# Rows of the rounded x at 512 columns instead of 528, for the first of two blocks

## The chip, the cores and the metric

One core of one Trainium2 chip runs the whole program. The metric is the device time of one execution in microseconds (us); the median over several runs is compared. An engine is named as in the profile: PE is TensorE (its matmuls), PEld its weight loads, DVE is VectorE, ACT is ScalarE, POOL is GpSimd, SP the queue that issues most DMAs.

## The reference, cut to what matters

Two blocks of a network, one after the other, on 512 tokens of width 1024, everything in float32.

```
# first block
u = rmsnorm(h, g_mix);  z = u @ w_in            # 7440 columns
y_gla, y_conv, y_swa = three mixers of parts of z, each @ its own output matrix
h = h + (sigmoid(gates0)*y_gla + sigmoid(gates1)*y_conv + sigmoid(gates2)*y_swa) @ w_o
u = rmsnorm(h, g_ffn);  hid = causal_dwconv(u @ w_up, ffn_conv_w)   # 2 x 2816 columns
h = h + (silu(hid[:2816]) * hid[2816:]) @ w_down
x2 = rmsnorm(h, g_final)
# second block: 16 meta tokens set ahead of x2 (528 tokens), two other mixers, another FFN
```

## The kernel before, in words

The activations lie with the model dimension on the 128 partitions: x is eight k-tiles of 128 rows of the model dimension, and in each partition a k-tile is one row of tokens. A float32 product is made of three float32r products: each operand is split into a rounded high part and a low part (the rest), and `pass3` (L181 through `mm`) issues weights-high by x-high, weights-high by x-low, weights-low by x-high, all into one accumulator of 512 columns. `gemm` does that for each k-tile of one group of 128 output columns: 8 k-tiles x 3 = 24 matmuls with 512 moving columns, and an evacuation by DVE and ACT afterwards.

The rounded x lives in two buffers `XH` and `XL` of 8 rows x 528 columns (`L` = 512 tokens + 16 meta tokens). The first block uses 512 columns of each row, from column `X1` = 8 on. The second block uses all 528. So row k begins k x 2112 bytes after the first.

The weights come from one stream in the order of use (`WStream`): 1024 columns (8 tiles of 128 columns, 512 bytes each in a partition) in one DMA into `wraw`, then ACT casts them to `wh` (L83) and DVE writes the rest to `wl` (L84). Three buffers each of `wh` and `wl` (4096 bytes a partition), two of `wraw`.

The buffers are laid out in a partition in the order of their allocation. Between the start of `XH` and the start of the first `wh` buffer lie XH and XL (16896 bytes each), the parameters (2048), the constants (1632) and two `wraw` (4096 each): 45664 bytes, which is 89 x 512 + 96. All weight tiles are whole multiples of 512 bytes from that one. `MH`/`ML` (the merged mixers' output, split), `bh_*`/`bl_*` (the mixers' outputs, split) and `FH`/`FL` (the hidden layer of the FFN, split) have rows of 512 columns (2048 bytes); their starts, from the sizes of the tiles ahead of them, are whole multiples of 512 bytes from the weights. `MH` begins 131072 + 96 bytes after `XH`, and `ML` as much after `XL`.

The order of work of the first block: a first group of four output tiles with x as the stationary operand, then 30 gemms of `w_in` among which the mixers' small matmuls are woven (`Lane`, `tick`: generators that are advanced after each k-tile), then 8 rounds of 3 gate gemms (24 matmuls each) and 3 gemms of the mixers' output matrices (4 k-tiles, 12 matmuls each), then `w_o` (8 gemms that read `MH`, `ML`), then the FFN: 44 gemms of `w_up` that read `XH`, `XL` and 8 gemms of `w_down` (22 k-tiles each) that read `FH`, `FL`. In the evacuation of `w_down` the second block's x is written into `XH`, `XL` (`after`). The matmuls of x with 512 moving columns are thus 30 + 24 + 44 = 98 gemms of 24.

Of the kernel before, what the change touches and what calls it, by code (L numbers as in the profile page):

```python
# [10 lines left out]
F32R = mybir.dt.float32r  # L11
# [7 lines left out]
P = 128  # L19
D = 1024  # L20
T = 512
META = 16
L = T + META
PADL = T + 32
X1 = 8
KD = D // P
NFF = 22
EPS = 1e-6
# [99 lines left out]
class Builder:  # L128
# [177 lines left out]
    def setup(self):  # L306
        nc, c = self.nc, self.const
        self.H = c.tile([P, KD, L], F32, name="H")
        self.XH = c.tile([P, KD, L], F32R, name="XH")
        self.XL = c.tile([P, KD, L], F32R, name="XL")  # L310
        self.par_t = c.tile([P, NPAR], F32, name="par_t")
        cm = c.tile([P, 3 * P + 24], F32, name="cm")
        self.four = cm[:, 3 * P:3 * P + 16]
        self.ident, self.le, self.ones = (cm[:, i * P:(i + 1) * P] for i in range(3))
        nc.scalar.preload_act_table_set("exp_and_others")
        nc.sync.dma_start(out=self.H[:, 0, META:L], in_=self.ins["xT"][:, 0])
        nc.scalar.dma_start(out=self.par_t[:, 0:8], in_=self.ins["par"][:, 0:8])
        self.W.load_to(0)
        for k in range(1, KD):
            nc.sync.dma_start(out=self.H[:, k, META:L], in_=self.ins["xT"][:, k])  # L320
            if k == 2:
                self.W.load_to(1)
        nc.gpsimd.dma_start(out=self.par_t[:, 8:NPAR], in_=self.ins["par"][:, 8:NPAR])
        nc.gpsimd.dma_start(out=cm[:, 0:3 * P + 16], in_=self.ins["cm"])
        nc.gpsimd.dma_start(out=self.H[:, :, 0:META], in_=self.ins["metaT"])

    def X(self, c0=META):
        return lambda k: (self.XH[:, k, :], self.XL[:, k, :])

    def sumsq(self, acc, k, src):  # L330
        if k == 0:
# [169 lines left out]

    def block1(self):
        nc, tc = self.nc, self.tc
        H, XH, XL = self.H, self.XH, self.XL
        self.W.prep_to(0)
        sums = [self.sq_acc(), self.sq_acc()]

# [9 lines left out]
            self.act(t, h, AF.Square)  # L517
            eng.tensor_tensor(out=sums[k % 2], in0=sums[k % 2], in1=t, op=ALU.add)
        for k in range(KD):
            self.split(XH[:, k, X1:X1 + T], XL[:, k, X1:X1 + T], H[:, k, META:L], self.par("g_mix", k))  # L520
            if k > 2:
                square(k - 3)
        for k in range(KD - 3, KD):
# [1 line left out]
        Rt = self.stat.tile([P, 4], F32, tag="Rt", name="Rt", bufs=1)  # L525
        R = self.r_tile()
        Rx = R[:, META:L]
        segs = [(X1, T)]
        X = self.X()
        WI = lambda c: [("w_in", k, c) for k in range(KD)]  # L530

        with ExitStack() as s1:
# [10 lines left out]
            with ExitStack() as s2:  # L543
# [14 lines left out]
                with tc.tile_pool(reuse_waits="tile", name="sp", bufs=1) as sp:  # L558
                    self.dist = sp.tile([P, 256], F32, name="dist")
                    nc.gpsimd.dma_start(out=self.dist, in_=self.ins["dist"])  # L560
                    sk = sp.tile([P, T], F32, name="sk")
                    svt = sp.tile([P, 4, P], F32, name="svt")
                    sq = [sp.tile([P, T], F32, name=f"sq{t}") for t in range(4)]
                    accs = [self.acc() for _ in range(4)]
                    for k in range(KD):
                        wh, wl = self.W.take([("w_in", k, GV + m * P) for m in range(4)])
                        for b in range(4):
                            c = slice(X1 + b * P, X1 + (b + 1) * P)
                            for i, (x, w) in enumerate(((XH, wh), (XL, wh), (XH, wl))):
                                self.mm(accs[b], x[:, k, c], w, start=k == 0 and i == 0, stop=k == 7 and i == 2)  # L570
                        if k == 5:
                            self.norm(self.token_rstd(sums, D, R, META, Rt), 4)
                        self.tick(4)

                    def ev_gv(a):
                        for b in range(4):
                            self.act(self.GVt[:, b, :], a[b], AF.Copy, scale=Rt[:, b:b + 1])
                    self.pend.append((ev_gv, accs))
                    self.flush(2)
                    self.lanes[1].add(self.meta_norm(), 6)  # L580
                    self.gemm16(wga, self.par("g_mix", 0, KD), [(META, T)], 3,
                                lambda a: self.mul(self.GAt[0:96], a[0][0:96], Rx[0:96]))
                    self.gemm(WI(SK), X, segs, lambda a: self.mul(sk, a[0], Rx))
                    sv = sp.tile([P, T], F32, tag="pT", name="sv", bufs=2)

                    def sv_gen():
                        ps = self.sm()
                        for n in range(4):
                            self.tr(ps[:, n * P:(n + 1) * P], sv[:, n * P:(n + 1) * P])
                        nc.scalar.copy(svt.rearrange("p a b -> p (a b)"), ps)  # L590
                        yield 1
                    self.gemm(WI(SV), X, segs, lambda a: self.mul(sv, a[0], Rx))
                    self.lanes[0].add(sv_gen(), 3)
                    for t in range(4):
                        self.gemm(WI(("sq", t)), X, segs,
                                  lambda a, t=t: self.stt(sq[t], a[0], 0.125, Rx, ALU.mult, ALU.mult))
                    self.flush(0, 1)
                    self.lanes[0].add(self.swa(sp, sq, sk, svt), 3)
                    sgr = [br.tile([P, T], F32, tag=f"blg{i}", name=f"sgr{i}") for i in range(4)]
                    for h in range(4):  # L600
                        def ev_gr(a):
                            t = gp.tile([P, T], F32, tag="a1", name="gr", bufs=1)
                            self.mul(sgr[h], a[0], Rx)
                            self.act(t, sgr[h], AF.Sigmoid)
                            self.mul(sgr[h], sgr[h], t)
                        self.gemm(WI(GR + h * P), X, segs, ev_gr)
                    glas = []
                    for h in range(4):
                        q = gp.tile([P, T], F32, tag="q", name="q", bufs=2)
                        kk = gp.tile([P, T], F32, tag="kk", name="kk", bufs=2)  # L610
                        self.gemm(WI(GQ + h * P), X, segs,
                                  lambda a: self.stt(q, a[0], float(P) ** -0.5, Rx, ALU.mult, ALU.mult))
                        self.gemm(WI(GK + h * P), X, segs, lambda a: self.mul(kk, a[0], Rx))
                        self.lanes[2].add(self.gla_head(gp, h, q, kk, sgr[h]), 2)
                    self.flush(0, 1)
# [48 lines left out]
            for m in range(KD):  # L664
                def ev_o(a, m=m):
                    h = H[:, m, META:L]
                    self.add(h, h, a[0])
                    self.split(XH[:, m, X1:X1 + T], XL[:, m, X1:X1 + T], h, self.par("g_ffn", m))
                    self.sumsq(sqa, m, h)
                self.gemm([("w_o", k, m * P) for k in range(KD)], lambda k: (MH[:, k, :], ML[:, k, :]), [(0, T)], ev_o)  # L670
        R = self.r_tile()
# [2 lines left out]
        g1 = self.stat.tile([P, 8], F32, tag="g1", name="g1", bufs=1)  # L674
        nc.gpsimd.tensor_tensor(out=g1, in0=self.par("g_final", 0, 8), in1=self.par("norm1", 0, 8), op=ALU.mult)

        def after(m, h, _):
            self.split(XH[:, m, META:L], XL[:, m, META:L], h, g1[:, m:m + 1])
            self.split(XH[:, m, 0:META], XL[:, m, 0:META], H[:, m, 0:META], self.par("norm1", m))
            self.sumsq(sqh, m, h)  # L680
            self.ts(h, h, self.par("g_final", m), ALU.mult)
            self.sumsq(sqg, m, h)
# [3 lines left out]
    def ffn(self, up, cw, cb, down, R, after, zero):  # L686
        nc, tc, H = self.nc, self.tc, self.H
        W = T + 2
        segs = [(X1, T)] if zero else [(META - 2, 256), (META + 254, 258)]
        rsegs = [(META, T)] if zero else segs  # L690
        Xb = (self.XH, self.XL)
        with tc.tile_pool(reuse_waits="tile", name="fp", bufs=1) as fp:
            FH = fp.tile([P, NFF, T], F32R, name="FH")
            fp.tile([P, P], F32, name="pad3")
# [1 line left out]
            for j in range(NFF):  # L696
                cs = []
                for i in range(2):
                    f = j + NFF * i
                    u = fp.tile([P, W], F32, tag="u", name="u", bufs=2)  # L700
                    c = fp.tile([P, T], F32, tag=f"c{i}", name=f"c{i}", bufs=2 if i == 0 else 1)
# [3 lines left out]
                    def ev(a, i=i, f=f, u=u, c=c, cs=cs, j=j):  # L705
# [13 lines left out]
                        else:  # L719
                            self.mul(c, cs[0], c)  # L720
                            self.split(FH[:, j, :], FL[:, j, :], c)
                    self.gemm([(up, k, f * P) for k in range(KD)],
                              lambda k: (Xb[0][:, k, :], Xb[1][:, k, :]), segs, ev)
                    cs.append(c)
            for m in range(KD):
                def ev_d(a):
# [338 lines left out]

    def block2(self, sqh, sqg):
        nc, tc, st = self.nc, self.tc, self.stat
        H, XH, XL = self.H, self.XH, self.XL
        W2 = T + 2
        R = self.r_tile()  # L1070

# [22 lines left out]
        self.norm(norm2(), 10)  # L1094
        segs = [(0, 264), (264, 264)]
        segq = [(META - 2, 256), (META + 254, 258)]
        X = self.X()
        WI = lambda c: [("w_in_2", k, c) for k in range(KD)]

        with ExitStack() as sy:  # L1100
# [406 lines left out]
```

## Time and profile before

| what | value |
|---|---|
| median of 3 runs | 1769.63 us (1768.66 to 1769.98) |
| profiled execution, its own time | 1771.67 us |
| its span (first to last instruction) | 1769.8 us |
| PE busy | 1738.0 us (98%) |
| DVE busy | 1089.8 us (62%) |
| ACT busy | 729.7 us (41%) |
| DMA, mean | 91 GB/s |
| mean granted TensorE clock | 0.997 |

The busy time of PE is the union of its matmuls, which overlap: the end of one runs into the next. So the pace of a stage is read from the starts of its matmuls, not from their durations. Around the span lie 1.87 us that the profile does not place.

### The profile page before, as it was taken

The numbers are of one execution on the slowest core, as the hardware profiler recorded it, in microseconds if no ns is written. First come the engines' busy times: TensorE is split into PE (matmuls) and PEld (weight loads), VectorE is DVE, ScalarE is ACT, GpSimd is POOL, SyncE is SP. The second block draws the span as 40 slices with busy tenths as digits, with TensorE's granted clock in tenths as the row PEclk, the third lists the DMA queues.
The fourth block names the chain that finished last, engine by engine and source line by source line (L and its number), as shares of the span: only waits on it lengthen the run. The fifth ranks groups of instructions, "written<-read, shape, count | busy, mean of one in ns | idle before, by whom it ended". The sixth has DMA issues, their size and how long they took to land. (4 is left out here: it accounts for less than half of the span.)

```text
span 1769.8 us, 26970 instructions
## 1 busy us (share of the span) xinstructions
PE 1738.0 (98%) x11014; PEld 1534.6 (87%) x11014; DVE 1089.8 (62%) x1923; ACT 729.7 (41%) x1175; POOL 123.9 (7%) x203
## 2 busy tenths in 40 slices
PE   8999999999999999999998999999999999999997
PEld 6777778888888888888897999999999999999885
DVE  4476774444457777734488789767643667766332
ACT  4355443222344444433356545545432444444221
POOL 2000000000110000001112221000001000000000
PEclk9999999999999999999999999999999999999999
DMA  5222223332333333233333322122223223332331
GB/s 184 84 72 60 64 80 96 96 96 95 96 95 94 93 94 95 92 100 101 88 101 126 113 86 72 61 73 72 72 84 96 84 96 95 86 95 96 96 89 67
DMA packets 45691, 160.84 MB, mean 91 GB/s; under 512 B 5472, under 2 KB 5616, under 8 KB 45568
## 3 DMA queue, kind: packets, MB, share of 16 engines
q1 hardware_dynamic: 42480, 149.83, 27.3%
q0 software_dynamic: 2800, 9.03, 1.6%
q8 instruction: 86, 1.41, 0.3%
q14 instruction: 37, 0.30, 0.1%
q10 hardware_dynamic: 288, 0.27, 0.0%
HBM read 156.93 MB, written 2.18 MB: 90 GB/s over the span
## 5 line engine op out<-in xcount | busy, mean ns | idle before, releaser
L181 PE MATMUL acc<-XH,wh 128*128 128x512 f32 (+3 forms) x2320 | 633.2, 326 | 0.1
L181 PE MATMUL acc<-XL,wh 128*128 128x512 f32 (+3 forms) x2320 | 621.1, 321 | 0.0
L181 PE MATMUL acc<-XH,wl 128*128 128x512 f32 (+3 forms) x2320 | 619.0, 320 | 0.0
L83 ACT CAST wh<-wraw 128x1024 fp32r<-128x1024 f32 (+1 forms) x279 | 292.0, 1047 | 507.8 <-PE acc L181 441.8
L84 DVE TENSOR_TENSOR wl<-wraw,wh 128x1024 fp32r<-128x1024 f32 (+1 forms) x279 | 342.6, 1228 | 218.8 <-ACT wh L83 211.4
L181 PEld LDWEIGHTS acc<-XH,wh 128*128 128x128 f32 x2320 | 385.1, 189 | 45.2 <-issue 9.8
L181 PEld LDWEIGHTS acc<-XH,wl 128*128 128x128 f32 x2320 | 385.3, 189 | 33.8 <-issue 0.5
L181 PEld LDWEIGHTS acc<-XL,wh 128*128 128x128 f32 x2320 | 385.9, 189 | 32.9 <-issue 0.5
L181 PE MATMUL acc<-FH,wh 128*128 128x512 f32 x352 | 137.8, 392 | 0.0
L181 PE MATMUL acc<-FH,wl 128*128 128x512 f32 x352 | 137.1, 390 | 0.0
L181 PE MATMUL acc<-FL,wh 128*128 128x512 f32 x352 | 137.0, 389 | 0.0
L164 DVE SCALAR_TENSOR_TENSOR c<-u,par_t,c 128x512 f32<-128x512 f32 x176 | 131.8, 749 | 6.7 <-ACT c L178 3.7
L152 DVE TENSOR_TENSOR u<-acc,R 128x512 f32<-128x512 f32 (+2 forms) x132 | 63.8, 510 | 87.9 <-PE acc L181 84.7
L336 POOL TENSOR_TENSOR sqa<-sqa,sqt 128x512 f32<-128x512 f32 x27 | 40.8, 1513 | 735.5 <-ACT sqt L178 735.5
L181 PEld LDWEIGHTS acc<-FH,wl 128*128 128x128 f32 x352 | 66.1, 188 | 14.0
L181 PEld LDWEIGHTS acc<-FL,wh 128*128 128x128 f32 x352 | 66.1, 188 | 13.5
L181 PEld LDWEIGHTS acc<-FH,wh 128*128 128x128 f32 x352 | 66.1, 188 | 13.4
L178 ACT ACTIVATE FH<-c 128x512 fp32r<-128x512 f32 x44 | 27.8, 632 | 116.0 <-DVE c L152 116.0
L178 ACT ACTIVATE c<-u,par_t 128x512 f32<-128x512 f32 x88 | 67.6, 768 | 2.4 <-DVE u L152 2.2
L152 DVE TENSOR_TENSOR H<-H,acc 128x512 f32<-128x512 f32 (+2 forms) x41 | 22.6, 569 | 74.6 <-PE acc L181 74.6
L178 ACT ACTIVATE c<-c 128x512 f32<-128x512 f32 x44 | 27.8, 632 | 83.5 <-DVE c L164 83.5
L181 PE MATMUL acc<-yh,wh 128*128 128x256 f32 (+1 forms) x256 | 51.4, 282 | 0.1
(393 smaller groups left out, 1967.1 us busy)
## 6 DMA issues: line engine op xcount, KB each, us to landing
wraw<-in_wts SPq DMA_DIRECT2D x277, 512.0 KB, 3.6
seg<-cumd POOLq DMA_DIRECT2D x10, 512.0 KB, 4.3
H<-in_xT SPq DMA_DIRECT2D x8, 256.0 KB, 9.6
ei<-eid POOLq DMA_DIRECT2D x16, 128.0 KB, 3.3
out<-H SPq DMA_DIRECT2D x7, 256.0 KB, 2.7
wraw<-in_wts SPq DMA_DIRECT2D x2, 256.0 KB, 4.6
r<-in_r POOLq DMA_DIRECT2D x1, 272.0 KB, 3.2
r<-in_r POOLq DMA_DIRECT2D x1, 256.0 KB, 8.3
```

Of the source, the lines that this page charges most:

```text
L83: self.nc.scalar.copy(h[:, e], t[:, e])
L84: self.nc.vector.tensor_tensor(out=l[:, e], in0=t[:, e], in1=h[:, e].bitcast(F32), op=ALU.subtract)
L152: self.nc.vector.tensor_tensor(out=out, in0=a, in1=b, op=op)
L164: self.nc.vector.scalar_tensor_tensor(out=out, in0=a, scalar=s, in1=b, op0=op0, op1=op1)
L178: self.nc.scalar.activation(out=out, in_=a, func=func, scale=scale, **kw)
L181: self.nc.tensor.matmul(out, lhsT, rhs, start=start, stop=stop)
L336: self.nc.gpsimd.tensor_tensor(out=acc, in0=acc, in1=t, op=ALU.add)
```

## The change

The two buffers keep their place and size. For the first block they are seen as 8 rows of 512 columns, from column 24 of the flat buffer on (`self.X1`, rows of 2048 bytes, the first 96 bytes in); for the second block as before, 8 rows of 528 columns (`self.X2`). All users take the view that they need. No instruction is added or taken away.

```diff
-X1 = 8
+X1 = 24
...
-        self.XH = c.tile([P, KD, L], F32R, name="XH")
-        self.XL = c.tile([P, KD, L], F32R, name="XL")
+        self.X1, self.X2 = [], []
+        for n in ("XH", "XL"):
+            x = c.tile([P, KD * L], F32R, name=n)
+            self.X1.append(x[:, X1:X1 + KD * T].rearrange("p (k t) -> p k t", t=T))
+            self.X2.append(x.rearrange("p (k t) -> p k t", t=L))
...
-    def X(self, c0=META):
-        return lambda k: (self.XH[:, k, :], self.XL[:, k, :])
+    def X(self, x):
+        return lambda k: (x[0][:, k, :], x[1][:, k, :])
...
-            self.split(XH[:, k, X1:X1 + T], XL[:, k, X1:X1 + T], H[:, k, META:L], self.par("g_mix", k))
+            self.split(XH[:, k, :], XL[:, k, :], H[:, k, META:L], self.par("g_mix", k))
...
-        segs = [(X1, T)]
-        X = self.X()
+        segs = [(0, T)]
+        X = self.X(self.X1)
...
-                            c = slice(X1 + b * P, X1 + (b + 1) * P)
+                            c = slice(b * P, (b + 1) * P)
...
         def after(m, h, _):
-            self.split(XH[:, m, META:L], XL[:, m, META:L], h, g1[:, m:m + 1])
-            self.split(XH[:, m, 0:META], XL[:, m, 0:META], H[:, m, 0:META], self.par("norm1", m))
+            self.split(XH2[:, m, META:L], XL2[:, m, META:L], h, g1[:, m:m + 1])
+            self.split(XH2[:, m, 0:META], XL2[:, m, 0:META], H[:, m, 0:META], self.par("norm1", m))
...
-        segs = [(X1, T)] if zero else [(META - 2, 256), (META + 254, 258)]
+        segs = [(0, T)] if zero else [(META - 2, 256), (META + 254, 258)]
...
-        Xb = (self.XH, self.XL)
+        X = self.X(self.X1 if zero else self.X2)
```

`block2` takes `self.X2` everywhere.

## Rows read from the trace of the kernel before

**Rows 1.** Busy time and count of each engine in seven stretches (windows view)

```profile
0.00:38.60 38.60, 31.48 (x137) 22.89 (x137) 19.39 (x32) 21.67 (x31) 12.60 (x19) 1.00 0.59 198
38.60:258.90 220.30, 216.60 (x1145) 171.49 (x1144) 146.02 (x303) 100.04 (x204) 0.40 (x4) 1.00 0.23 72
258.90:458.20 199.30, 199.30 (x868) 162.18 (x867) 94.26 (x114) 58.29 (x71) 0.00 (x0) 1.00 0.31 95
458.20:501.70 43.50, 43.50 (x194) 36.03 (x193) 21.15 (x25) 17.09 (x24) 11.23 (x8) 1.00 0.31 97
501.70:748.20 246.50, 246.50 (x1073) 200.03 (x1072) 175.89 (x236) 107.92 (x141) 6.02 (x43) 1.00 0.30 94
748.20:867.90 119.70, 119.70 (x529) 99.09 (x528) 49.16 (x50) 37.21 (x46) 16.94 (x12) 1.00 0.31 97
867.90:1769.80 901.90, 880.93 (x7079) 842.86 (x7078) 583.96 (x1165) 387.48 (x661) 76.74 (x117) 0.99 0.28 88
```

**Rows 2.** Groups by form, whole span: one of three passes over x, first block

```profile
L181 PE MATMUL acc<-XH,wh 128*128 128x512 f32 x784 | 312.5, 399 | 0.0
```

**Rows 3.** Timeline of PE, two starts in w_up, 960 matmuls apart

```profile
514.69 0.39 PE L181 MATMUL acc<-XH,wh 128*128 128x512 f32 x1
...
737.09 0.39 PE L181 MATMUL acc<-XH,wh 128*128 128x512 f32 x1
```

**Rows 4.** Timeline of PE, two starts in w_o, 180 matmuls apart

```profile
458.84 0.39 PE L181 MATMUL acc<-MH,wh 128*128 128x512 f32 x1
...
499.64 0.39 PE L181 MATMUL acc<-MH,wh 128*128 128x512 f32 x1
```

**Rows 5.** Timeline of PE, start of w_down: matmuls 0, 4, 10 and 500

```profile
748.21 0.39 PE L181 MATMUL acc<-FH,wh 128*128 128x512 f32 x1
...
749.15 0.39 PE L181 MATMUL acc<-FL,wh 128*128 128x512 f32 x1
...
750.53 0.39 PE L181 MATMUL acc<-FL,wh 128*128 128x512 f32 x1
...
861.60 0.39 PE L181 MATMUL acc<-FH,wl 128*128 128x512 f32 x1
```

**Rows 6.** Timeline of PE, gate rounds: matmuls 0, 108, 120 and 144

```profile
300.59 0.39 PE L181 MATMUL acc<-bh_gla,wh 128*128 128x512 f32 x1
...
325.49 0.39 PE L181 MATMUL acc<-bh_gla,wh 128*128 128x512 f32 x1
...
328.26 0.39 PE L181 MATMUL acc<-bh_conv,wh 128*128 128x512 f32 x1
...
333.70 0.39 PE L181 MATMUL acc<-XH,wh 128*128 128x512 f32 x1
```

**Rows 7.** Timeline of PE, second block's w_down, after four small matmuls

```profile
1649.30 0.60 PE L184 MATMUL sm<-cm,H 128*128 128x128 f32 x4
...
1651.36 0.39 PE L181 MATMUL acc<-FL,wh 128*128 128x512 f32 x1
...
1654.99 0.39 PE L181 MATMUL acc<-FH,wl 128*128 128x512 f32 x1
```

**Rows 8.** Timeline of PE in w_in, first and last of 96 matmuls without small ones

```profile
53.10 0.48 PE L181 MATMUL acc<-XH,wh 128*128 128x512 f32 x1
...
75.22 0.39 PE L181 MATMUL acc<-XH,wl 128*128 128x512 f32 x1
```

**Rows 9.** Waits of PE in w_in, the two longest in total

```profile
PE sm L181 <- DVE b L152: 1.5, 2, 0.8
PE sm L184 <- DVE p L168: 1.3, 1, 1.3
```

**Rows 10.** The page's DMA issues: the weight stream

```profile
wraw<-in_wts SPq DMA_DIRECT2D x277, 512.0 KB, 3.6
```

**Rows 11.** Groups in w_up: the weights' cast and what it waits for

```profile
L83 ACT CAST wh<-wraw 128x1024 fp32r<-128x1024 f32 x44 | 46.3, 1053 | 40.7 <-PE acc L181 37.8 <-issue 2.9
```

**Rows 12.** Windows view, second block, the stretch with a lowered granted clock

```profile
960.00:983.00 23.00, 19.34 (x158) 17.87 (x158) 18.32 (x26) 14.55 (x34) 6.71 (x9) 0.93 0.32 115
```

More of the change, by code (lines that the diff above doesn't have):

```diff
@@ L503, in block1 @@
         nc, tc = self.nc, self.tc
-        H, XH, XL = self.H, self.XH, self.XL
+        H, (XH, XL), (XH2, XL2) = self.H, self.X1, self.X2
         self.W.prep_to(0)
@@ L667, in ev_o @@
                     self.add(h, h, a[0])
-                    self.split(XH[:, m, X1:X1 + T], XL[:, m, X1:X1 + T], h, self.par("g_ffn", m))
+                    self.split(XH[:, m, :], XL[:, m, :], h, self.par("g_ffn", m))
                     self.sumsq(sqa, m, h)
@@ L722, in ffn @@
                     self.gemm([(up, k, f * P) for k in range(KD)],
-                              lambda k: (Xb[0][:, k, :], Xb[1][:, k, :]), segs, ev)
+                              X, segs, ev)
                     cs.append(c)
@@ L1067, in block2 @@
         nc, tc, st = self.nc, self.tc, self.stat
-        H, XH, XL = self.H, self.XH, self.XL
+        H, (XH, XL) = self.H, self.X2
         W2 = T + 2
@@ L1096, in block2 @@
         segq = [(META - 2, 256), (META + 254, 258)]
-        X = self.X()
+        X = self.X(self.X2)
         WI = lambda c: [("w_in_2", k, c) for k in range(KD)]
```

## The prediction

> **What bounds the kernel now.** I read the windows by stage first. In the three stages after `w_in` and in `w_down`, PE is busy without a gap (199.30 of 199.30 us, 43.50 of 43.50, 246.50 of 246.50, 119.70 of 119.70) at the full granted clock, while DVE has 71% at most (175.89 of 246.50) [rows 1]. In `w_in` itself PE still has 216.60 of 220.30 us. So in the first block the time is the number of matmuls times the distance between their starts, and nothing else. Busy time hides that distance, since a matmul of 0.39 us overlaps its successor; the timeline shows it.
>
> There the reader is to see two paces for one and the same matmul (128x128 weights, 512 moving columns). In `w_up`, where x is moving, 960 matmuls take 737.09 − 514.69 = 222.40 us, 231.7 ns each [rows 3]. In `w_o`, where `MH`/`ML` are moving, 180 take 40.80 us, 226.7 ns each [rows 4]. In `w_down`, after its beginning, 490 take 861.60 − 750.53 = 111.07 us, 226.7 ns again [rows 5]. Weights, accumulators and clock are the same in the three. What differs is where the moving row lies: `MH`, `ML`, `FH`, `FL` have every row a whole multiple of 512 bytes from the weight tiles, while row k of x begins, from column 8 on and 2112 bytes apart, at 64 − 64k bytes modulo 512 from them.
>
> The pace does not follow the address at once. When `w_down` takes over from `w_up`, its first ten matmuls take 750.53 − 748.21 = 2.32 us, 232 ns each, and only then the pace is 226.7 [rows 5]. In the gate rounds the first output gemm after the gates reads aligned rows (`bh_gla`) too, and its twelve matmuls take 2.77 us, 231 ns each; the next 24 take 5.44 us, 226.7 ns [rows 6]. After four small matmuls in the second `w_down` the fast pace is back by the eighth matmul: 16 in 3.63 us from there [rows 7]. So aligned rows give the fast pace after some ten undisturbed matmuls, and any other row loses it.
>
> **The change part by part.** It adds and removes no instruction; it moves addresses. With the first row 96 bytes in and rows of 2048 bytes, the distance from an x row to a weight tile is 45664 − 96 = 89 x 512 bytes less k x 2048, a multiple of 512 for every k, in `XL` too (16896 = 33 x 512). More than that: the rows are those of `MH` and `ML` moved by exactly 131072 bytes, read with the same weight buffers in the same order of passes. The row that prices the new matmul is therefore that of `w_o`, 226.7 ns; the far bound on the other side is an aligned row in its slow beginning, 749.15 − 748.21 = 0.94 us for four, 235 ns [rows 5]. I take 226.7, as all three aligned operands arrive there.
>
> All 784 matmuls of each pass [rows 2], 2352 in all, would save 2352 x 5.0 ns = 11.8 us if each were settled; that is the upper bound. By stage:
>
> - `w_up`: 44 gemms, 1056 matmuls. Some 25 at its start stand around the norm's 16 small matmuls. 1030 x 5.0 ns = 5.2 us.
> - Gate rounds: a round of 108 matmuls now takes 325.49 − 300.59 = 24.90 us [rows 6]. All aligned, it takes 108 x 226.67 ns = 24.48 us. The gemm of `bh_gla` gains with it, since its predecessor no longer disturbs it. 8 x 0.42 = 3.4 us.
> - The 30 gemms of `w_in`, 720 matmuls, woven with small ones. Undisturbed, x runs here as elsewhere: 96 matmuls have 95 steps in 22.12 us [rows 8], 233 ns with the slow first step. Bounds: nothing, if no stretch settles; 720 x 5.0 ns = 3.6 us, if all do. Along the timeline I counted the stretches: the ten longest between small matmuls hold 472 matmuls, the one shown being the longest, and less ten each for settling 372 are left; the others are mostly under ten. 372 x 5.0 ns = 1.9 us.
> - The start of `w_down` is entered settled: ten matmuls save 0.05 us. The first group, with x stationary, waits for the splits of x; I put it at nothing.
>
> The sum is 5.2 + 3.4 + 1.9 + 0.05 = 10.5 us.
>
> What must keep up with a PE that is 2.2% faster? The weights: 24 matmuls use up one load, 24 x 226.7 ns = 5.44 us, and a load lands 3.6 us after its issue [rows 10]; the cast of the next weights waits 37.8 us in `w_up` for PE to free a buffer [rows 11], so the stream is ahead and has slack. DVE goes from 71% to 175.89 / 241.3 = 73% in `w_up`. In `w_in` PE waits a few times for DVE in the mixers' chains, 1.5 and 1.3 us in the two largest rows [rows 9]; there a faster PE just waits longer, and a part of the 1.9 us may go. I take off nothing for it; the whole term is the price.
>
> Hazards between the views: the second block's row m of `XH` now lies across rows m − 1 and m of the first block's x. It is written in the evacuation of `w_down`, after the last `w_up` gemm has read x, as before; the 16 meta columns overlapped the old row as well (columns 8 to 15). So the wait that guards it ends at the same gemm. The second block reads the same addresses as before, and its 901.90 us [rows 1] should stay. One thing there can move by chance: a stretch of 23 us has a mean granted clock of 0.93 [rows 12], a short fall to the lower level (1.2 GHz) after PE had gaps, worth at most 0.07 x 23 = 1.6 us; whether it falls there again 10 us earlier is open.
>
> One rule speaks against all of this. The rows show x and `MH` 5 ns apart with nothing else changed [rows 3, 4]. The Trainium skill, page "TensorE: Matmul & The Clock Gate", section "Step-by-step: what each phase is for", gives TensorE two independent read ports in SBUF, one for the moving operand and one for the weights, and the page "SBUF — State Buffer", section "SBUF: two separate sides", says that PE never waits on another reader. By these the place of x could not matter, and the sum would be 0. The trace disagrees so far, by those 5 ns.
>
> **The rivals.**
>
> *The address is not the cause (no change).* The moving buffers could differ in the work around them: DVE is busier in `w_up` (71%) than in `w_down` (49.16 of 119.70, 41%) [rows 1], and DVE and ACT write SBUF all the time. Then x stays at 231.7 ns and the time at 1769.6 us. For it: no aligned operand was seen with so busy a DVE. Against it: in one gate round, under the same work, the pace goes from 231 to 226.7 ns as the operand changes [rows 6]. The two independent read ports of the Trainium skill's page named above would have it come out this way.
>
> *Only part settles.* If x settles in the gate rounds but DVE's density in `w_up` upsets it, or if `w_in` gives nothing and `w_up` half, the gain is 3.4 to 6 us: 1763.6 to 1766.2 us. Against it: the pace in `w_up` is the same over 960 matmuls, among evacuations, casts and DMAs alike.
>
> *Aligned rows stick at the slow state (slower).* Rows 2048 bytes apart put every row of x into the same relation to the weights. If that were a bad one, every matmul would pay: at 235 ns, 3.3 ns more than now, 2352 x 3.3 ns = 7.8 us, 1777.4 us. It decides at the point where the ten slow matmuls of [rows 5] do not end. For it: aligned rows do begin at 235 ns, slower than x. Against it: each aligned operand seen left that state within twelve matmuls, and `MH` shares the very addresses modulo 131072.
>
> **How the numbers follow.** The sum is against the profiled execution: 1771.67 − 10.5 = 1761.2 us by its own time. It ran 2.04 us above the median of the runs, so the forecast for a median is 1769.63 − 10.5 = 1759.1 us. Its own range: 11.8 us saved and 0.7 us of run spread below (1757.1), `w_in` giving nothing and the clock's fall in the worse place above (1769.6 − 8.6 + 1.6 = 1762.6). Chances: forecast 0.80, part 0.08, no change 0.07, slower 0.05. The forecast's own range holds the 8 in 10, so it is the range. A change under 0.2% (3.5 us) is about what a measurement of this kernel cannot tell from none; the part rival ends just beyond it, in most of its span. Faster 0.87, same 0.08, slower 0.05.
>
> **What would show it.** Right: `w_up` lasts 241.3 us instead of 246.5, with 226.7 ns between starts; a gate round 24.48 us; the first ten matmuls of `w_down` at 226.7 ns; in `w_in` the long stretches at 226.7 ns after about ten matmuls, the short ones unchanged; `w_o`, `w_down` and the second block as long as now. Wrong in the sum: DVE or ACT shown as what PE waits for in `w_up`. Wrong altogether: x rows still with uneven steps near 232 ns, or steady ones at 233 ns or more.

## The result, and the profile after

The changed kernel takes 1760.57 us in the median of 4 runs (1757.49 to 1762.2), the kernel before 1769.61 us beside it: 0.9948 of it, 95% interval 0.993 to 0.9965. With more runs of both, in the first experiment, it is 1759.64 us (5 runs) against 1770.28 us (15 runs), 0.9941 (0.9927 to 0.9954). The forecast was 1759.1 us, 1757.1 to 1762.6.

The profiled execution is the fastest of the first four (1757.49 us, span 1755.6 us). Its stages, cut at the same instructions as [rows 1], in the windows view (length, then busy time and count of PE, PEld, DVE, ACT, POOL, granted clock, DMA share, GB/s):

```profile
0.00:37.10 37.10, 30.16 (x137) 22.10 (x137) 19.52 (x33) 21.60 (x32) 13.71 (x19) 1.00 0.61 206
37.10:255.67 218.57, 214.25 (x1145) 171.30 (x1144) 145.71 (x303) 100.07 (x204) 0.40 (x4) 1.00 0.24 73
255.67:451.84 196.17, 196.08 (x868) 162.11 (x867) 94.32 (x114) 58.42 (x71) 0.00 (x0) 1.00 0.31 97
451.84:495.34 43.50, 43.50 (x194) 36.02 (x193) 21.16 (x25) 17.10 (x24) 11.22 (x8) 1.00 0.31 97
495.34:736.72 241.38, 241.38 (x1073) 199.89 (x1072) 175.74 (x235) 107.82 (x140) 6.02 (x43) 1.00 0.31 96
736.72:856.37 119.65, 119.65 (x529) 99.09 (x528) 49.19 (x50) 37.22 (x46) 16.95 (x12) 1.00 0.32 97
856.37:1755.60 899.23, 879.39 (x7079) 841.52 (x7078) 583.64 (x1165) 387.19 (x661) 76.86 (x117) 1.00 0.28 88
```

Against [rows 1]: start −1.50 us, `w_in` −1.73, gate rounds −3.13, `w_o` 0, `w_up` −5.12, `w_down` −0.05, second block −2.67. The counts of matmuls are the same, their order too (in all ten traces of this document the 11014 matmuls come in one and the same order), and `w_up` is still PE from end to end; only the step between matmuls has shrunk.

The timeline of PE shows the step. In `w_up`, the same two matmuls as in [rows 3], 960 apart:

```profile
508.25 0.39 PE L181 MATMUL acc<-XH,wh 128*128 128x512 f32 x1
...
725.85 0.39 PE L181 MATMUL acc<-XH,wh 128*128 128x512 f32 x1
```

217.60 us, 226.7 ns each, where it was 231.7. At the entry into `w_down`, matmuls 0 and 10 of [rows 5]:

```profile
736.73 0.39 PE L181 MATMUL acc<-FH,wh 128*128 128x512 f32 x1
...
739.00 0.39 PE L181 MATMUL acc<-FL,wh 128*128 128x512 f32 x1
```

2.27 us for ten instead of 2.32: the stream comes in settled. In the gate rounds, matmuls 0, 108 and 120 of [rows 6]:

```profile
296.76 0.39 PE L181 MATMUL acc<-bh_gla,wh 128*128 128x512 f32 x1
...
321.24 0.39 PE L181 MATMUL acc<-bh_gla,wh 128*128 128x512 f32 x1
...
323.96 0.39 PE L181 MATMUL acc<-bh_conv,wh 128*128 128x512 f32 x1
```

A round takes 24.48 us (24.90 before), and the twelve matmuls of the first output gemm 2.72 us (2.77), though their own operand was not moved. In `w_in`, the long stretch of [rows 8], its matmuls 0, 10 and 95:

```profile
51.43 0.48 PE L181 MATMUL acc<-XH,wh 128*128 128x512 f32 x1
...
53.82 0.39 PE L181 MATMUL acc<-XL,wh 128*128 128x512 f32 x1
...
73.09 0.39 PE L181 MATMUL acc<-XH,wl 128*128 128x512 f32 x1
```

After the small matmuls the first ten still take 2.39 us, 239 ns each with the slow first step; the other 85 take 19.27 us, 226.7 ns. The settling is there, as in `w_down` before. But `w_in` has waits as well. The waits of PE in this stage, the third row of the kernel before (the other two are [rows 9]) and then all of the changed kernel (us in total, times, longest):

```profile
PE sm L181 <- ACT a L456: 0.8, 1, 0.8
...
PE sm L181 <- DVE b L152: 1.6, 2, 0.9
PE sm L184 <- DVE p L168: 1.5, 1, 1.5
PE sm L181 <- ACT a L459: 0.9, 1, 0.9
PE sm L181 <- DVE k L152: 0.3, 1, 0.3
```

They add up to 3.6 us before and 4.3 us after: a part of what the steps save is waited away.

Last, the place in the second block that answers to [rows 12], in the windows view:

```profile
945.00:968.00 23.00, 20.20 (x178) 18.93 (x177) 20.66 (x29) 14.07 (x33) 6.84 (x9) 1.00 0.43 145
```

The granted clock is whole here; in this execution it did not fall in this part.

### The profile page after: what moved, and what is told of

The parts are those of the page before. It is cut to its first block, busy times and chain, and to the rows that moved or that the text cites. A ratio compares the mean times of both kernels' runs of the same rounds, so it can differ in the third digit from the quotient of the medians.

```text
span 1755.6 us, 26969 instructions
## 1 busy us (share of the span) xinstructions
PE 1724.4 (98%) x11014; PEld 1532.0 (87%) x11014; DVE 1089.3 (62%) x1923; ACT 729.4 (42%) x1175; POOL 125.2 (7%) x203
```

## The experiments

**The changed kernel again**, no edit.

> The changed kernel once more, unedited, to part what the change gives from what an execution gives by chance. Theory (aligned rows settle): the first block repeats within 0.1 us from the first gemm of w_in to the end of w_down: w_in 1.9 us, gate rounds 2.9 us, w_up 5.1 us shorter than before, about 10 us together; the 1.5 us at the start and the 2.9 us in the second block of the first profile belong to falls of the granted clock and need not come again. So 1759 to 1762 us in the median. Rival (the start and the second block gained from the change too): both come again, 1755 to 1757 us.

1759.64 us (1758.46 to 1759.72). Windows view, the start, `w_in`, gate rounds and `w_up`, cut as above, and the stretch of the second block with a lower clock:

```profile
0.00:37.41 37.41, 30.24 (x137) 22.21 (x137) 19.52 (x33) 21.75 (x32) 13.62 (x19) 1.00 0.62 204
37.45:256.00 218.55, 214.20 (x1145) 171.34 (x1144) 145.75 (x303) 100.11 (x204) 0.40 (x4) 1.00 0.24 73
256.00:452.15 196.15, 196.06 (x868) 162.15 (x867) 94.35 (x114) 58.45 (x71) 0.00 (x0) 1.00 0.32 97
495.65:737.04 241.39, 241.39 (x1073) 199.90 (x1072) 175.76 (x235) 107.81 (x140) 6.05 (x43) 1.00 0.32 96
...
930.00:960.00 30.00, 27.06 (x220) 24.69 (x217) 25.91 (x34) 17.17 (x37) 9.72 (x13) 0.94 0.39 123
```

The three stages repeat within 0.02 us. Against [rows 1] they are 1.75, 3.15 and 5.11 us shorter, 10.0 us together as expected, though not split as expected (1.9 and 2.9 for the first two). The clock fell this time. The part of the second block from the end of `w_down` to its output product, in the kernel before, in its second trace (below), in the first profile of the changed kernel and in this one:

```profile
867.94:1281.73 413.79, 405.34 (x3580) 390.75 (x3579) 321.93 (x765) 219.82 (x444) 55.57 (x104) 1.00 0.28 86
...
867.11:1280.30 413.19, 405.42 (x3581) 390.70 (x3580) 321.81 (x765) 219.59 (x444) 55.55 (x104) 1.00 0.28 86
...
856.41:1267.30 410.89, 403.83 (x3581) 389.43 (x3579) 321.70 (x765) 219.59 (x444) 55.66 (x104) 1.00 0.28 87
...
856.73:1269.45 412.72, 405.44 (x3581) 390.82 (x3579) 321.75 (x765) 219.60 (x444) 55.62 (x104) 1.00 0.28 86
```

The changed kernel differs from itself by 1.83 us here, with the fall and without; with the fall in both, it lies 0.5 to 1.1 us under the kernel before. So most of the first profile's gain there was chance. Of the start I had expected the same, and that was not so: it is short again (37.41 us); see the last two experiments.

**One relation for all k-tiles, but 64 bytes off.**

```diff
-X1 = 24
+X1 = 8
```

> Rows of 512 columns, but from column 8 instead of 24: every k-tile has one and the same relation to its weights, 64 bytes off a multiple of 512. Theory A (the row must be a whole multiple of 512 bytes from the weights): x never settles, 231 to 236 ns in w_up, 246 to 249 us for w_up, 1769 to 1773 us. Theory B (it is enough that the relation is the same for all k-tiles): 226.7 ns, w_up 241.4 us, 1760 us as the changed kernel. On ACT and DVE this one has the order of the kernel before, since the first row again lies over the first meta columns; if the start of the program gained by the order, its first gemm of w_in starts at 38.5 us again, else near 37 us.

1772.85 us (11 runs), 1.0016 of the kernel before (1.0007 to 1.0025): slower than both. `w_up` in the windows view:

```profile
501.94:750.14 248.20, 248.20 (x1073) 200.20 (x1072) 176.03 (x236) 107.29 (x141) 6.05 (x43) 1.00 0.31 94
```

and its timeline, two starts 960 apart, with the first few between them:

```profile
514.95 0.40 PE L181 MATMUL acc<-XH,wh 128*128 128x512 f32 x1
515.19 0.39 PE L181 MATMUL acc<-XL,wh 128*128 128x512 f32 x1
515.42 0.40 PE L181 MATMUL acc<-XH,wl 128*128 128x512 f32 x1
515.65 0.39 PE L181 MATMUL acc<-XH,wh 128*128 128x512 f32 x1
...
738.95 0.40 PE L181 MATMUL acc<-XH,wh 128*128 128x512 f32 x1
```

224.00 us for 960, 233.3 ns each. The same relation for all k-tiles is not what helps; theory B falls. A constant wrong relation costs 1.7 ns a matmul more (1.60 us in 960) than the mixed ones of before, which pass a good one at k = 1 and 5. The first gemm of `w_in` starts at 37.57 us, neither at 38.5 nor near 37: the start decided nothing here.

**Only the high part aligned.**

```diff
-            self.X1.append(x[:, X1:X1 + KD * T].rearrange("p (k t) -> p k t", t=T))
             self.X2.append(x.rearrange("p (k t) -> p k t", t=L))
+            self.X1.append(x[:, X1:X1 + KD * T].rearrange("p (k t) -> p k t", t=T)
+                           if n == "XH" else self.X2[1][:, :, 8:8 + T])
```

> XH in rows of 512 columns, aligned; XL as before, rows of 528 columns from column 8. Theory (one pass in three that is out of place keeps the stream from settling): w_up between, 243 to 246.5 us, with steps that still vary from k-tile to k-tile. Rival (each matmul has its own cost by its own row): two thirds of the gain, w_up 243.1 us, and steps next to XH rows at 226.7 ns.

One run, 1769.87 us. `w_up` in the windows view:

```profile
499.88:746.93 247.05, 247.05 (x1073) 200.01 (x1072) 176.05 (x236) 107.60 (x140) 6.06 (x43) 1.00 0.32 94
```

Two starts in it, 960 matmuls apart:

```profile
512.86 0.40 PE L181 MATMUL acc<-XH,wh 128*128 128x512 f32 x1
...
735.79 0.40 PE L181 MATMUL acc<-XH,wh 128*128 128x512 f32 x1
```

222.93 us, 232.2 ns each, where 226.7 was the settled step. Not two thirds of the gain, but none: 0.55 us more than before, outside the range that I had written. One pass in three out of place keeps the whole stream from settling. The cost of a matmul is not its own row's alone.

**Another operand put out of place.**

```diff
-            MH = mp.tile([P, KD, T], F32R, name="MH")
-            mp.tile([P, P], F32, name="pad2")
+            MH = mp.tile([P, KD * L], F32R, name="MH").rearrange("p (k t) -> p k t", t=L)[:, :, 0:T]
```

> The changed kernel with MH, the high part of what w_o reads, in rows of 528 columns (first row aligned, the others 64 bytes more out of place each); ML stays. The second block's work comes out in another order in this program, so only the first block is read. Theory (the place of the moving row decides): w_o, 43.5 us before and after, becomes 44.0 to 44.7 us, uneven steps. Rival (x gained for another reason than its place, say the work around it): w_o stays at 43.5 us.

`w_o` and `w_up` in the windows view:

```profile
451.76:496.41 44.65, 44.65 (x193) 36.02 (x192) 21.17 (x25) 17.14 (x24) 11.17 (x8) 1.00 0.32 94
496.43:737.78 241.35, 241.35 (x1073) 199.90 (x1072) 175.76 (x235) 107.82 (x140) 6.00 (x43) 1.00 0.32 96
```

Two starts in `w_o`, 180 matmuls apart as in [rows 4]:

```profile
452.42 0.40 PE L181 MATMUL acc<-MH,wh 128*128 128x512 f32 x1
...
494.32 0.40 PE L181 MATMUL acc<-MH,wh 128*128 128x512 f32 x1
```

The settled stage of before loses its pace when its rows are moved, 44.65 us for 43.50 and 232.8 ns a step for 226.7, with DVE and ACT as busy as they were and the DMA nearly so (94 GB/s for 97); `w_up`, which was not touched here, keeps 241.35. So the place of the row is the cause, in both directions. The whole program took 1760.61 us in its one run.

**256 and 128 bytes off.**

```diff
-X1 = 24
+X1 = 88    # 256 bytes off
...
-X1 = 24
+X1 = 56    # 128 bytes off
```

> Rows of 512 columns from column 88: every row 256 bytes off a multiple of 512 from the weights. Theory A (a multiple of 512 is needed): no settling, w_up 246 to 249 us as at 64 bytes off. Theory A2 (a multiple of 256 is enough; the steps of the kernel before repeat from k-tile k to k+4, which is 256 bytes): 226.7 ns, w_up 241.4 us.

> Rows of 512 columns from column 56: every row 128 bytes off. Theory A and A2: w_up 246 to 249 us. If a multiple of 128 bytes were enough: 241.4 us.

`w_up` in the windows view, 256 bytes off:

```profile
495.81:737.17 241.36, 241.36 (x1073) 200.00 (x1072) 175.79 (x235) 107.72 (x140) 6.03 (x43) 1.00 0.31 96
```

and 128 bytes off:

```profile
501.21:748.45 247.24, 247.24 (x1073) 200.66 (x1072) 175.88 (x235) 107.36 (x140) 6.03 (x43) 1.00 0.31 94
```

A multiple of 256 bytes is enough (A2); 128 is not. The totals, one run each: 1759.97 and 1770.04 us, with 1769.83 us for the kernel before beside them.

**The start: the kernel before again, and aligned rows with the order of before.** A scheduler sets the order of ACT and DVE. In the changed kernel the first row no longer overlaps the first 16 meta columns (its 64 bytes lie ahead of it), so their split is moved to the start of the program, and a cast of weights comes earlier. The second edit keeps the overlap and aligns by a pad:

```diff
-X1 = 24
+X1 = 8
...
+        c.tile([P, 112], F32, name="pad4")
         self.par_t = c.tile([P, NPAR], F32, name="par_t")
```

> The kernel before, unedited, for a second trace of its start. If the start of the first gemm of w_in at 38.56 us in the first trace was set by the order of ACT and DVE or by the rows' place, it comes again within 0.3 us; if by the moment at which TensorE's clock rose, it moves with that moment (11.7 us there).

> Aligned rows of 512 columns, from column 8, with a pad of 448 bytes ahead of the weights so that the distance is a multiple of 512 all the same. The first row then lies over the first meta columns, and the start of the program has the order of the kernel before on ACT and DVE (later parts come out in another order, so only the start and w_up are read). Theory: w_up 241.4 us, as it is the place that counts and not the column. If the order made the start shorter, its first gemm starts at 38 to 38.6 us; if the place of the rows did, at 37 to 37.4 us.

Windows view of the start in the kernel before, second trace, and then its stretch from 6 to 14 us:

```profile
0.00:37.65 37.65, 30.34 (x137) 21.89 (x137) 19.36 (x32) 21.78 (x31) 11.63 (x19) 1.00 0.61 203
...
6.00:14.00 8.00, 7.91 (x26) 5.66 (x26) 3.71 (x5) 4.67 (x7) 3.13 (x6) 1.00 1.02 367
```

Aligned rows with the order of before, the same two stretches and `w_up`:

```profile
0.00:38.10 38.10, 31.49 (x136) 22.92 (x136) 19.38 (x32) 21.79 (x31) 11.62 (x19) 1.00 0.61 200
...
496.35:737.71 241.36, 241.36 (x1073) 199.95 (x1072) 175.92 (x236) 107.93 (x141) 6.02 (x43) 1.00 0.32 96
...
6.00:14.00 8.00, 8.00 (x22) 6.03 (x23) 3.12 (x5) 4.20 (x7) 3.12 (x6) 1.00 1.03 369
```

`w_up` takes 241.36 us with column 8 and a pad: it is the distance that counts, not the column. The totals of the two, one run each, were 1770.18 and 1757.85 us.

The start is less clear. The kernel before itself starts `w_in` at 38.56 us in one trace and 37.65 in the other, so 0.9 us of the first profile's 1.50 can come by chance, three times the 0.3 us that I had allowed. Executions differ in how many matmuls they get through between 6 and 14 us, 26 and 22 in the two above, but that does not order their starts: 128 bytes off there are 22 too, and `w_in` starts at 37.45 us.

All ten traces together say more. Four have the order of the kernel before: out of place 38.56, 37.65 and 37.57 us (64 bytes off), aligned 38.10. Six have the new order of ACT at the start: in place 37.06, 37.41, 36.99 (`MH` moved) and 37.58 (256 bytes off), out of place 37.08 (only the high part aligned) and 37.45 (128 bytes off). Within either order the place of the rows shows no effect on the start; the new order starts 0.7 us earlier in the mean. The two groups touch at 37.57, so with four and six traces this is likely the order, as the 38.10 us of the aligned program with the old order were to tell, but it is not shown.

## Why the prediction was right, point by point

- *The path.* PE's step is the time of the first block: shown. `w_up` became 241.38 us, with 241.3 forecast, and PE waits for nothing in it.
- *The price of a settled matmul*, taken from the row of `w_o` [rows 4]: 226.7 ns, as forecast.
- *The sum.* `w_up` 5.12 us for 5.2; gate rounds 3.13 for 3.4, as the first round is still broken by small matmuls; `w_down` 0.05 for 0.05. `w_in` gave 1.73 us for 1.9, and here two errors cancel in part. The ten longest stretches saved 2.1 us (they hold 478 matmuls in the trace, not 472) and the shorter ones, put at nothing, 0.2 us; some 0.6 us of that went again, as the waits of PE grew from 3.6 to 4.3 us. I had named these waits and taken off nothing. Together the stages gave 10.03 us for 10.5. The start, put at nothing, may give some 0.7 us, by the order on ACT and DVE and not by the place of the rows. Between medians the runs measured 9.0 and 10.6 us.
- *The rule of two ports.* The Trainium skill, page "TensorE: Matmul & The Clock Gate", section "Step-by-step: what each phase is for", has separate ports for the moving operand and the weights. That may hold, but it does not follow that the place of the row is free: `MH` moved alone, two passes of the three, costs 1.15 us in 192 matmuls. Here the measurement decides.
- *No change* fell with the experiment on `MH`: the work around is the same and the pace changes. *Only part* fell with `w_up` at 226.7 ns under DVE's 73%. *Slower* did not come with this change, but its mechanism exists: 64 bytes off, one relation for all k-tiles is slower than before, 233.3 ns a step. Its price of 235 ns was too high: it was read from two starts only four matmuls apart, and the first ten of the same [rows 5] give 232. With the buffers where they lie, the start column decides on which side such a change ends.
- *The alignment needed* was argued as a multiple of 512 bytes, because all rows that settled had that. It is 256. The steps of before could have told: in the mean over the 960 matmuls of [rows 3], the three passes of k-tile 0 take 228.0, 233.5 and 233.5 ns, those of k-tile 1 225.9, 235.5 and 228.5, and k-tiles 4 and 5, 256 bytes further, have the same within 0.1 ns.
- *The clock's fall in the second block*, bounded at 1.6 us: between two traces of the changed kernel, with the fall and without, it is 1.83 us (412.72 and 410.89), so the bound was a little small. The 2.9 us between the first two profiles are not the fall alone: the traces shown that both have it still differ by up to 1.1 us. Of the 14.2 us between the first two spans, some 4 us are this part and the start, most of it chance.

What makes the pace depend on the distance between the row that streams and the weights is not settled. The runs show the dependence, that 0 and 256 bytes settle where 64 and 128 do not, and that it is a property of the stream and not of one matmul.

## What to carry to other kernels

Where a stage is matmuls back to back, read the step between their starts and compare stages with the same shape: two paces for one shape point to the operands' place. Put the rows of the moving operand, in all passes of the stream, at a multiple of 256 bytes from the weights; one operand out of place spoils it for all. A fixed row length alone doesn't do it: a wrong start column is then wrong for every row. All this is shown for one shape, 128x128 weights and 512 moving columns of float32r with new weights for every matmul; for other shapes and types it has to be measured.

## What the runs showed that I had not expected

- With 512 moving columns an aligned stream steps at 226.7 ns; every stream that was out of place stepped at 231.7 (mixed), 233.3 (64 bytes off) or 232.4 ns (128 bytes off, `w_up` 247.24 us), also when two passes of three were aligned (232.2 ns, `w_up` 247.05 us).
- A disturbance by small matmuls costs a settled stream some ten steps at 231 to 239 ns, and those of an unsettled one cost about the same (the first ten of [rows 8] took 2.42 us before and 2.39 after); so the gain falls where the stream is cut often: 5.12 us for the 1056 matmuls of `w_up`, 1.73 for the 720 of `w_in`.
- The same kernel's time varies from run to run, and with the clock: the kernel before ran between 1767.58 and 1773.62 us in 15 runs, the three at a mean granted clock of 0.998 between 1768.26 and 1768.51, the two at 0.995 at 1772.32 and 1773.62.
